# Loading the first rows of a position table on a second DMA ring, beside the indices of an embedding gather

## The chip, the core and the metric

The kernel runs on one core of a Trainium2 chip. A core has a matrix engine (PE), VectorE (DVE), ScalarE (ACT), GpSimd (POOL) and SyncE (SP), and 16 DMA engines that move data between HBM and on-chip memory. SyncE, ScalarE and GpSimd can each issue DMAs; here each of the three has a ring (queue) of its own, which feeds the same 16 DMA engines.

The metric is device time in microseconds (us) of one launch. Kernels are compared only with runs of the kernel before on the same chip.

## The reference

```python
batch, seq_len, vocab_size, d_model = 32, 512, 50000, 512
def reference(indices, embedding_table, position_embed):
    return (embedding_table[indices] + position_embed).astype(np.float32)
```

There are 32 x 512 = 16384 rows of 2 KB to gather, add to and store: 33.55 MB in and 33.55 MB out. The positions (1.05 MB) and the indices (0.13 MB) are small beside that.

## The kernel before

A batch of 512 positions lies as 128 partitions x 4 rows (`k` = 0 to 3), so one indirect DMA gathers 128 rows, 256 KB, with one index per partition. There are 128 gathers. The first 16 (batches 0 to 3) take their indices from a small tile, `idx0`, that is loaded directly; they run in the order of all `k` = 0, 1 first, then all `k` = 2, 3. The later ones take theirs from a transposed tile that the engines make meanwhile. VectorE adds the positions, which ScalarE has copied to PSUM, and SyncE stores.

```python
    # SyncE: loads, then (below) all stores
        nc.sync.dma_start(out=idx0[:], in_=idx_first).then_inc(s_first, 16)   # 16 KB
        load_pos(0)                                  # k = 0, 1: 512 KB
        nc.sync.wait_ge(s_pos[0], 16)
        load_pos(1)                                  # k = 2, 3: 512 KB
        nc.sync.dma_start(out=idx_raw[:], ...).then_inc(s_raw, 16)            # 128 KB
    # GpSimd
        nc.gpsimd.wait_ge(s_first, 16)
        for g, (b, k) in enumerate(order):
            # ... (waits for the transposed indices and for free slots)
            ins = nc.gpsimd.indirect_dma_start(
                out=slots[b % SLOTS][:, k, :], ..., in_=table,
                in_offset=bass.IndirectOffsetOnAxis(ap=where, axis=0),
            ).then_inc(s_gather[g % LANES], 16)
    # VectorE, for each gather (cut)
            if b == 0:
                nc.vector.wait_ge(s_ps, k + 1)
            nc.vector.tensor_tensor(out=part, in0=part, in1=pos_ps[:, k, :], op=add
            )._wait_ge(s_gather[g % LANES], rounds(g)).then_inc(s_add, 1)
    # ScalarE
        for k in range(K):
            nc.scalar.copy(out=pos_ps[:, k, :], in_=pos_sb[:, k, :])._wait_ge(
                s_pos[k // half], 16).then_inc(s_ps, 1)
    # SyncE: stores of 512 KB (two k of a batch), waiting on s_add
```

## Time and profile before

| | kernel before |
|---|---|
| time, median of 3 runs | 183.18 us (183.13 to 183.28) |
| the profiled run | 177.2 us, span 175.5 us (6 us under the timed runs) |
| first gather starts | 3.31 us |
| last gather starts | 162.31 us |
| gathers | 128, one every 1.25 us |
| busy share | GpSimd 69%, VectorE 51%, DMA engines over 90% nearly throughout |

These are whole lines from the page of the profile. The first three are by slice: each digit or number is one of 40 equal slices of the span, in tenths of busy time or in GB/s. The last two are the chain of waits that ended last, by engine and by line of the program.

```profile
POOL 4777777777777777777777777777777777777200
DMA  4799999999999999999999999999999999999993
GB/s 120 234 316 309 349 383 402 390 410 410 416 412 418 416 419 419 418 418 418 416 421 418 420 418 420 418 418 419 418 416 417 420 418 418 418 419 418 418 413 130
...
POOL 66%; issue 24%; DMA 5%; POOLq 1%; DVE 0%; SPq 0%
POOL slot L131 66%; DMA slot<-in_embedding_table_dram,idx_t 4%; DMA idx<-in_indices_dram 1%; POOLq L139 1%; DVE slot L166 0%; POOLq L126 0%; SPq L211 0%; SPq L103 0%
```

The last gather in that chain, from its start to its landing (start, duration, what):

```profile
162.31 7.63 DMA slot<-in_embedding_table_dram,idx_t
```

The timeline of the head, before. Columns: start, duration, engine ("SPq" is a DMA being issued by SyncE), line, operation, out<-in, count, and in brackets how long the engine sat idle before it and what ended that.

```profile
1.02 0.43 SPq L105 DMA_DIRECT2D idx<-in_indices_dram  x1
1.52 3.83 SPq L99 DMA_DIRECT2D pos_sb<-in_position_embed_dram  x2
3.31 1.14 POOL L131 DMA_INDIRECT slot<-in_embedding_table_dram,idx  x1 [1.72 <-DMA idx<-in_indices_dram]
5.03 1.11 ACT L172 COPY pos_ps<-pos_sb 128x512 f32<-128x512 f32 x2 [2.77 <-DMA pos_sb<-in_position_embed_dram]
6.79 0.69 DVE L166 TENSOR_TENSOR slot<-slot,pos_ps 128x512 f32<-128x512 f32 x1 [6.79 <-DMA slot<-in_embedding_table_dram,idx]
...
10.85 0.69 DVE L166 TENSOR_TENSOR slot<-slot,pos_ps 128x512 f32<-128x512 f32 x1 [3.37 <-DMA slot<-in_embedding_table_dram,idx]
```

The first gather waits for the indices alone. The positions, behind them on the same ring, arrive while the gather is under way: the first add (6.79) waits for the gather, not for them.

### The profile page before, as it was taken

How to read it: one execution, taken by the hardware profiler on the slowest of the kernel's cores; microseconds unless marked ns; L12 is line 12 of the kernel's file. 1: busy time of each engine (PE TensorE's matmuls, PEld its weight loads, DVE VectorE, ACT ScalarE, POOL GpSimd, SP SyncE). 2: the span in 40 equal slices, each digit the busy share in tenths (PEclk: the TensorE clock that was granted, in tenths of full speed). 3: DMA queues.
4: the chain of work that ended last, by engine and by line, in shares of the span. 5: the costliest groups of instructions: out<-in, count | busy, mean ns of one | idle time of the engine just before them, and what ended most of it. 6: DMA issues, size and time to landing. Idle time of an engine off the chain costs nothing.

```text
span 175.5 us, 423 instructions
## 1 busy us (share of the span) xinstructions
PE 1.0 (1%) x4; PEld 0.4 (0%) x4; DVE 89.1 (51%) x133; ACT 3.5 (2%) x5; POOL 121.9 (69%) x134
## 2 busy tenths in 40 slices
PE   0000100000000000000000000000000000000000
PEld 0000000000000000000000000000000000000000
DVE  0136645555465556465545554565455645554550
ACT  2220000000000000000000000000000000000000
POOL 4777777777777777777777777777777777777200
DMA  4799999999999999999999999999999999999993
GB/s 120 234 316 309 349 383 402 390 410 410 416 412 418 416 419 419 418 418 418 416 421 418 420 418 420 418 418 419 418 416 417 420 418 418 418 419 418 418 413 130
DMA packets 20851, 68.34 MB, mean 389 GB/s; under 512 B 3696, under 2 KB 3824, under 8 KB 20848
## 3 DMA queue, kind: packets, MB, share of 16 engines
q1 hardware_dynamic: 10608, 34.76, 49.0%
q0 software_dynamic: 10240, 33.56, 49.0%
q14 instruction: 3, 0.02, 0.0%
HBM read 34.75 MB, written 33.55 MB: 389 GB/s over the span
## 4 chain that ended last, share of the span: by engine, by line
POOL 66%; issue 24%; DMA 5%; POOLq 1%; DVE 0%; SPq 0%
POOL slot L131 66%; DMA slot<-in_embedding_table_dram,idx_t 4%; DMA idx<-in_indices_dram 1%; POOLq L139 1%; DVE slot L166 0%; POOLq L126 0%; SPq L211 0%; SPq L103 0%
## 5 line engine op out<-in xcount | busy, mean ns | idle before, releaser
L131 POOL DMA_INDIRECT slot<-in_embedding_table_dram,idx_t x112 | 105.9, 946 | 34.1 <-issue 34.1
L166 DVE TENSOR_TENSOR slot<-slot,pos_ps 128x512 f32<-128x512 f32 x128 | 87.9, 688 | 81.5 <-DMA slot<-in_embedding_table_dram,idx_t 63.6
L131 POOL DMA_INDIRECT slot<-in_embedding_table_dram,idx x16 | 15.3, 958 | 6.3 <-issue 4.6
L172 ACT COPY pos_ps<-pos_sb 128x512 f32<-128x512 f32 x4 | 2.2, 586 | 8.0 <-DMA pos_sb<-in_position_embed_dram 8.0
L172 ACT ACT_TABLE_LOAD x1 | 1.3, 1283 | 1.0 <-SPq L103 1.0
L160 DVE CAST idx_t<-turned 32x128 int32<-32x128 f32 x4 | 1.1, 279 | 0.1
L144 PE MATMUL turned<-ident,idx_f 128*32 128x128 f32 x4 | 1.0, 416 | 17.2 <-DVE idx_f L154 17.2
L114 POOL MEMSET ones<- 128x128 f32 x1 | 0.2, 204 | 0.5 <-SPq L103 0.5
L144 PEld LDWEIGHTS turned<-ident,idx_f 128*32 128x32 f32 x4 | 0.4, 133 | 17.3 <-DVE idx_f L154 17.2
L115 POOL TENSOR_SCALAR_AFFINE_SELECT ident<-ones 128x128 f32<-128x128 f32 x1 | 0.3, 287 | 0.1
L200 POOL MEMSET const-float32-0.0<- 128x1 f32 x1 | 0.1, 98 | 0.3 <-issue 0.3
L154 DVE CAST idx_f<-idx_raw 128x128 f32<-128x128 int32 x1 | 0.2, 220 | 0.0
L200 POOL MEMSET const-uint8-127<- 128x1 uint8 x1 | 0.1, 115 | 0.0
L200 POOL MEMSET const-bfloat16-1.0<- 128x1 bf16 x1 | 0.1, 109 | 0.0
L200 POOL MEMSET const-float32-1.0<- 128x1 f32 x1 | 0.1, 101 | 0.0
## 6 DMA issues: line engine op xcount, KB each, us to landing
out_dram<-slot SPq DMA_DIRECT2D x61, 512.0 KB, 6.6
slot<-in_embedding_table_dram,idx_t POOLq DMA_INDIRECT x112, 7.4
out_dram<-slot SPq DMA_DIRECT2D x6, 256.0 KB, 3.9
pos_sb<-in_position_embed_dram SPq DMA_DIRECT2D x2, 512.0 KB, 4.9
slot<-in_embedding_table_dram,idx POOLq DMA_INDIRECT x16, 6.3
idx_raw<-in_indices_dram SPq DMA_DIRECT2D x1, 128.0 KB, 6.2
idx<-in_indices_dram SPq DMA_DIRECT2D x1, 16.0 KB, 2.0
```

Of the source, the lines that this page charges most:

```text
L114: nc.gpsimd.memset(ones[:], 1.0).then_inc(s_ident, 1)
L115: nc.gpsimd.affine_select(out=ident[:], in_=ones[:], pattern=[[-1, P]], compare_op=mybir.AluOpType.is_equal, fill=0.0, base=0, channel_mul ...
L131: ins = nc.gpsimd.indirect_dma_start(out=slots[b % SLOTS][:, k, :], out_offset=None, in_=table, in_offset=bass.IndirectOffsetOnAxis(ap=whe ...
L139: nc.gpsimd.drain()
L144: ins = nc.tensor.transpose(turned[:, k].rearrange("p b j -> p (b j)"), idx_f[:, :, k], ident[:])
L154: nc.vector.tensor_copy(out=idx_f[:].rearrange("r p k -> r (p k)"), in_=idx_raw[:, :, 0])._wait_ge(s_raw, 16).then_inc(s_cast, 1)
L160: nc.vector.tensor_copy(out=idx_t[j * Q : (j + 1) * Q, :, :], in_=turned[:, :, :, j]).then_inc(s_idx, 1)
L166: nc.vector.tensor_tensor(out=part, in0=part, in1=pos_ps[:, k, :], op=add)._wait_ge(s_gather[g % LANES], rounds(g)).then_inc(s_add, 1)
L172: nc.scalar.copy(out=pos_ps[:, k, :], in_=pos_sb[:, k, :])._wait_ge(s_pos[k // half], 16).then_inc(s_ps, 1)
L200: nc = _bacc.Bacc("TRN2", target_bir_lowering=False, num_devices=1)
```

## The change

The intent: start the first gather sooner, by gating it on a quarter of the early indices; take the first positions off SyncE's ring so that they go out at the same moment; spread the later positions; and move the raw indices ahead of them.

```diff
-        if (b == 0 and k < half) or b == B - 1:
+        if (b <= 1 and k < half) or b == B - 1:
             stores.append((g + 1, b, k, 1))
...
-        nc.sync.dma_start(out=idx0[:], in_=idx_first).then_inc(s_first, 16)
-        load_pos(0)
-        nc.sync.wait_ge(s_pos[0], 16)
-        load_pos(1)
+        for k in range(half):
+            load_pos(nc.scalar, k)
+        nc.sync.dma_start(out=idx0[:, 0, :], in_=idx_first[:, 0, :]).then_inc(
+            s_first, 16
+        )
+        nc.sync.dma_start(out=idx0[:, 1:, :], in_=idx_first[:, 1:, :]).then_inc(
+            s_next, 16
+        )
         nc.sync.dma_start(
             out=idx_raw[:], in_=idx_rows.rearrange("r (s w) -> r s w", w=2)
         ).then_inc(s_raw, 16)
+        nc.sync.wait_ge(s_pos[half - 1], 16)
+        load_pos(nc.sync, half)
+        nc.sync.wait_ge(s_gather[0], 16)
+        load_pos(nc.sync, half + 1)
...
         for g, (b, k) in enumerate(order):
+            if g == half:
+                nc.gpsimd.wait_ge(s_next, 16)
```

(`load_pos` now takes an engine and one `k`, 256 KB, and ScalarE's copies wait for one semaphore per `k`.)

## The prediction

> **What bounds the kernel.** The page's DMA rows: the 16 DMA engines are at least 90% busy from the third of 40 slices to the last but one, at about 418 GB/s once settled. Bytes (34.75 MB read, 33.55 MB written) are the least the task allows, but for 1.2 MB of positions and indices. GpSimd keeps the same pace: in the timeline a gather starts every 1.25 us (0.95 busy, 0.30 "issue"), and 256 KB in plus 256 KB out per 1.25 us is 419 GB/s. The chain of waits names GpSimd (66%, issue 24%), but the last gather, issued at 162.31, takes 7.63 us to land where the quickest took 3.5 (DMA view of the gather line), so some 4 us of transfers are queued: DMA bounds the end, GpSimd is nearly level. Nothing between 20 and 170 us can gain. The head can: by slice it moves 120, 234, 316, 309, 349, 383 GB/s. Against 418 these slices of 4.39 us lose about 8.4 us, over 2 of them before any data moves.
>
> **What the change does.**
> 1. Only batch 0's indices (4 KB, not 16 KB) gate the first gather. Before, all took 2.01 us to land and the gather started at 3.31. The quarter should land sooner, but two 256 KB position loads now go out on ScalarE's ring at the same moment (ScalarE was free at 0.97, SyncE at 1.02). The Trainium skill ("DMA: Bandwidth & Descriptors", Issuing engines are not separate DMA queues) says that DMAs of different issuers share the same 16 engines and interleave; before issues every load from SyncE, so its trace cannot show this. The effects should nearly cancel: first gather 0.2 us earlier, between 0.5 earlier and 0.4 later.
> 2. Positions 0 and 1 no longer queue behind the indices (one SyncE issue: 0.43 us): the first ScalarE copy moves from 5.03 to about 4.2. It gates nothing: the first add waited until 6.79 for gather 0.
> 3. Raw indices (128 KB) move ahead of the later positions and fill the hole between the first positions and the first gather's data (DMA share 0.48 from 4 to 6 us), worth 0.3 to 0.5 us of transfers.
> 4. Positions 2 and 3 come as two 256 KB loads, the second after gather 0. Before, 512 KB plus 128 KB stood beside gathers 1 to 3: gather 1 (issued 4.75) was added only at 10.85. Now that add should come near 9. Batch 1's first pair is stored in two pieces, so writes mix with reads about 2 us sooner.
>
> Costs: three more DMAs (0.43 us of issue each, off the chain) and 2 KB packets instead of 4 KB for 1.5 MB. VectorE, TensorE and the gathers are unchanged.
>
> **Sum.** Only DMA idleness removed in the first 12 us counts: 0.4 (hole) + 0.2 (earlier gather) + 0.3 (earlier stores) = 0.9 us, an estimate. The end moves as much, since the queue of 4 us shrinks without emptying.
>
> **Predicted:** 182.3 us, 8 in 10 between 181.2 and 183.3. Faster by over 2%: 0.03; within 2%: 0.95; slower by over 2%: 0.02.
>
> **Signs.** First gather near 3.1; gather pace still 1.25; second add near 9; second slice above 234 GB/s; settled slices still 418; last gather's latency about 7 us.
>
> **What would make it wrong.** Position packets hold up the index slice (first gather after 3.5): no gain. If the timed runs, 6 us longer than the profiled one (177.2), spend that in the head, the gain could be larger; if GpSimd alone sets the end, only the first gather's shift counts.

## The result

| | before | changed |
|---|---|---|
| time, median of 4 runs each, same rounds | 183.16 us | 184.75 us |
| ratio | | 1.0085 (95% interval 1.0068 to 1.0103) |
| first gather starts (profile) | 3.31 us | 4.53 us |
| last gather starts | 162.31 us | 163.50 us |
| last data moved by a DMA engine | 173.15 us | 174.03 us |

A ratio is the mean time of one kernel's fast runs over the mean of the other's fast runs of the same rounds, so it is not quite the ratio of the medians quoted beside it. The change is a small loss, within 2% but clear of noise, and outside the predicted range of 181.2 to 183.3.

The page's lines after the change:

```profile
POOL 1877777777777777877877877877877777760000
DMA  4689999999999999999999999999999999999700
GB/s 143 178 282 351 368 368 367 397 410 412 416 418 418 415 422 418 417 425 416 418 423 415 419 422 413 424 418 417 424 415 418 424 416 420 421 415 423 298 2 0
...
POOL 60%; issue 23%; DMA 6%; DVE 4%; POOLq 1%; SPq 0%
```

The slices are longer here (183.7 us in 40 parts), because this profile ends with 9.7 us in which nothing moves; the zeros on the right are that end. It is no part of the change, as the runs below show. The settled rate is the same, about 418 GB/s. What differs is the left edge, GpSimd's 1 where it had 4.

The timeline of the head, after:

```profile
0.97 0.88 ACTq L98 DMA_DIRECT2D pos_sb<-in_position_embed_dram  x2
1.02 0.38 SPq L107 DMA_DIRECT2D idx<-in_indices_dram  x1
1.47 0.42 SPq L110 DMA_DIRECT2D idx<-in_indices_dram  x1
...
4.10 1.29 ACT L182 COPY pos_ps<-pos_sb 128x512 f32<-128x512 f32 x2 [0.93 <-DMA pos_sb<-in_position_embed_dram]
4.53 1.14 POOL L141 DMA_INDIRECT slot<-in_embedding_table_dram,idx  x1 [2.94 <-DMA idx<-in_indices_dram]
...
7.93 0.59 ACT L182 COPY pos_ps<-pos_sb 128x512 f32<-128x512 f32 x1 [2.55 <-DMA pos_sb<-in_position_embed_dram]
...
8.53 0.69 DVE L176 TENSOR_TENSOR slot<-slot,pos_ps 128x512 f32<-128x512 f32 x1 [8.53 <-ACT pos_ps L182]
...
9.86 0.69 DVE L176 TENSOR_TENSOR slot<-slot,pos_ps 128x512 f32<-128x512 f32 x1 [0.64 <-DMA slot<-in_embedding_table_dram,idx]
```

The view names ScalarE's copy as what released the first add at 8.53. By the program that add needs only the first copy, which was done by 4.7; the copy that ended at 8.52 is the third (`k` = 2). So it is the gather that the add waited for, as the repeat of this kernel says (e5, add at 8.33).

The index load is a quarter of the size and takes longer. One line of the chain of waits from each kernel, before and then after, gives it (start, duration, what):

```profile
1.02 2.01 DMA idx<-in_indices_dram
```

```profile
1.02 3.22 DMA idx<-in_indices_dram
```

The packet records of the two traces (one record for each piece that a DMA engine moves) show why. They were counted per quarter microsecond over all 16 DMA engines, by the ring's number and the record's size: 32 bytes are indices, 2048 and 4096 bytes are positions.

```
start (us)   before: SyncE's ring alone       changed: SyncE's ring | ScalarE's ring
1.94         49 x 32 B                                              | 14 x 2048 B
2.19         350 x 32 B                       4 x 32 B              | 16 x 2048 B
2.44         113 x 32 B,  5 x 4096 B          20 x 32 B             | 24 x 2048 B
2.69                     11 x 4096 B          32 x 32 B             | 28 x 2048 B
2.94                     19 x 4096 B          33 x 32 B             | 34 x 2048 B
3.19                     22 x 4096 B          26 x 32 B             | 41 x 2048 B
3.44                     18 x 4096 B          15 x 32 B             | 43 x 2048 B
```

Before, all 512 index records were gone in about 0.6 us and the positions followed, in order. After, the 128 records of the small slice come out between those of the positions, in the middle nearly one for one, for 1.3 us: by the start of the 128th, 194 position records of 2 KB had started. (Records of the second slice look the same, so this is the 128th on the ring.) These counts mix 16 engines, which the records do not name, but the nanoseconds show the turns: of the first 128 index records, 83 start 3 or 4 ns before a 2 KB record ends and have another 2 KB record start 5 or 6 ns after them. With the index times shifted by eight amounts between 17 and 60 ns, chance gives 6 to 23. An index record takes 7 to 9 ns; the 2 KB records beside it take 87 to 154 ns on average, and the slice has to wait through one at about two steps in three. The Trainium skill says, in "DMA: Bandwidth & Descriptors", Queues, rings and completion order, that each DMA engine goes round-robin between the rings that have work for it. This trace agrees as to taking turns. Turns are not the whole delay: the first index record itself comes later, at 2.35 and after 23 position records, where in the kernel before it started at 2.10. In e2 that part is larger.

So there is a theory with two steps. First, the position packets on the second ring hold up the index slice by over a microsecond. Second, the start of the first gather passes to the end nearly in full, because GpSimd then issues one gather per 1.25 us to the end: from first to last gather it takes 159.00 us before and 158.97 us after.

The rivals: the loss comes from the other parts (2 KB records, gated later loads, one store cut in two); or the ring on ScalarE is itself slow; or the delayed slice just shares bandwidth with all bytes in flight; and, against the second step, the DMA engines bound the end, as the prediction had it.

### The profile page after: what moved, and what is told of

Its sections match the earlier page's. It is cut to its first block, busy times and chain, and to the rows that moved or that the text cites. A ratio compares the mean times of both kernels' runs of the same rounds, so it can differ in the third digit from the quotient of the medians.

```text
span 183.7 us, 427 instructions
## 1 busy us (share of the span) xinstructions
PE 1.0 (1%) x4; PEld 0.4 (0%) x4; DVE 89.2 (49%) x133; ACT 3.6 (2%) x5; POOL 121.9 (66%) x134
## 4 chain that ended last, share of the span: by engine, by line
POOL 60%; issue 23%; DMA 6%; DVE 4%; POOLq 1%; SPq 0%
POOL slot L141 60%; DMA slot<-in_embedding_table_dram,idx_t 4%; DVE slot L176 4%; DMA idx<-in_indices_dram 2%; POOLq L149 1%; POOLq L136 0%; SPq L221 0%; SPq L102 0%
```

## The experiments

Twelve kernels ran, each on one chip with 11 runs of the kernel before beside them. "us" is (ratio - 1) times the median of before on that chip (177.58, 183.38 and 177.16 us); the gather's shift is against the 3.31 us of the first profile.

| run | first gather (us) | shift | ratio to before, 95% interval | us |
|---|---|---|---|---|
| e1 ScalarE waits for the slice | 3.00 | -0.31 | 0.9990 (0.9947 to 1.0033) | -0.2 |
| e2 before, only the ring changed | 5.04 | +1.73 | 1.0101 (1.0060 to 1.0141) | +1.8 |
| e3 before, only the slice split | 3.08 | -0.23 | 0.9977 (0.9940 to 1.0015) | -0.4 |
| e4 before again | 3.33 | +0.02 | 0.9986 (0.9945 to 1.0026) | -0.2 |
| e5 change again | 4.32 | +1.01 | 1.0065 (1.0049 to 1.0082) | +1.2 |
| e6 slice ahead on the same ring | 2.94 | -0.37 | 0.9992 (0.9973 to 1.0010) | -0.1 |
| e7 before, gather held back | 5.85 | +2.54 | 1.0137 (1.0115 to 1.0159) | +2.5 |
| e8 change without small stores | 4.49 | +1.18 | 1.0066 (1.0049 to 1.0083) | +1.2 |
| e9 half the positions beside | 4.20 | +0.89 | 1.0054 (1.0019 to 1.0090) | +1.0 |
| e10 short position records | 3.45 | +0.14 | 1.0028 (0.9986 to 1.0070) | +0.5 |
| e11 before, 512 KB less | 3.18 | -0.13 | 1.0012 (0.9970 to 1.0054) | +0.2 |
| e12 e6 again, another chip | 2.90 | -0.41 | 0.9970 (0.9933 to 1.0006) | -0.5 |

In every row the two columns, shift and us, agree within 0.4 us, in e11 too, which moves less data. The intervals are 0.3 to 0.8 us wide to each side, so this is as close as they can show.

### e1: ScalarE waits for the index slice

```diff
+        nc.scalar.wait_ge(s_first, 16)
         for k in range(half):
             load_pos(nc.scalar, k)
```

> The changed kernel, but ScalarE issues its two position loads only when the first index slice has landed. Theory (position packets on ScalarE's ring hold up the index slice): slice lands in under 2.0 us, first gather at or below 3.1 us in the profile instead of 4.53, and the run is at least 1.2 us faster than the changed kernel, so 183.5 us or less, at or below the kernel before. Rival (the loss comes from the smaller position loads, their gates or the extra small stores, the late gather being absorbed by the queue of transfers): gather early all the same, but time stays at 184.3 us or more.

```profile
3.00 1.14 POOL L142 DMA_INDIRECT slot<-in_embedding_table_dram,idx  x1 [1.42 <-DMA idx<-in_indices_dram]
```

The first gather started at 3.00 us. The chip was another than the first one, with before at 177.58, so the absolute numbers of the expectation could not be read; against before the run came to 0.9990, where the change stands at 1.0065 to 1.0085. The ring, the smaller loads, their gates and the small stores are all still there, so none of them is the loss.

### e2: the kernel before with its first positions on ScalarE's ring

```diff
-        load_pos(0)
+        load_pos(0, nc.scalar)
```

> The kernel before, with one edit: its first 512 KB position load goes out on ScalarE's ring, not behind the indices on SyncE. Theory: the 16 KB of indices now interleave with position packets, 32 descriptors a DMA engine against 8 of 4 KB; first gather after 4.0 us instead of 3.31, time 0.6 to 1.5 us above the kernel before. Rival (smaller loads, gates, small stores): none of these is here, so time within 0.3 us of the kernel before.

This one edit alone costs 1.8 us, slightly more than the expectation's upper end of 1.5. The gather starts at 5.04, later than in the changed kernel, since four times as many index records wait:

```profile
5.04 1.14 POOL L131 DMA_INDIRECT slot<-in_embedding_table_dram,idx  x1 [3.46 <-DMA idx<-in_indices_dram]
```

The last index record started at 4.41 us, after all 128 position records of 4 KB: 16 KB of indices came in behind 512 KB of positions although the two were issued within 0.05 us of each other (positions by ScalarE at 0.98, indices by SyncE at 1.02).

Taking turns is only part of it here. The first index record starts at 3.09, after 74 of the position records, where in the kernel before it started at 2.10. So 0.99 of the gather's 1.73 us are gone before the first turn. Why the second ring comes in so late, and later beside 4 KB records than beside 2 KB ones (2.35 in the changed kernel), is open; no run tried it.

### e3: the kernel before with the slice split off

```diff
-        nc.sync.dma_start(out=idx0[:], in_=idx_first).then_inc(s_first, 16)
+        nc.sync.dma_start(out=idx0[:, 0, :], in_=idx_first[:, 0, :]).then_inc(s_first, 16)
+        nc.sync.dma_start(out=idx0[:, 1:, :], in_=idx_first[:, 1:, :]).then_inc(s_next, 16)
...
+            if g == half:
+                nc.gpsimd.wait_ge(s_next, 16)
```

> The kernel before, with one edit: batch 0's indices (4 KB) are loaded by themselves ahead of those of batches 1 to 3, all on SyncE ahead of the positions. Theory: first gather at 2.9 to 3.1 us instead of 3.31, time 0.1 to 0.5 us below the kernel before. Rival (the start of the first gather does not set the end): gather as early, time the same within 0.1 us.

The gather starts 0.23 us sooner, and the ratio of 0.9977 has 1 in its interval. The part of the change that was meant to help does move the gather, by too little to be seen in the time on this chip.

### e4: the kernel before, again

> The kernel before, unchanged, as a control: ratio 1.000 within 0.002. Its profiled run of before was 177.2 us where its other runs were 183.1, and the changed kernel's profile ends with 9.6 us in which no data moves. If that slow end is in every ordinary run and the first profile just missed it, this profile shows some 8 us after the last store here too; if it comes from the change, it does not.

Ratio 0.9986, as a control should be. Its profile shows no slow end (span 175.1 us, last data at 172.90), but all runs of this chip were near 177 us, so this could not answer the question about the end. That answer came from e6 and e12.

### e5: the change, again

> The changed kernel unchanged, as a control beside the kernel before on one chip. First gather at 4.4 to 4.6 us as before; 0.7 to 1.7 us slower than the kernel before (the prediction's own run said 1.6). On a chip without the slow end its span ends within 2.5 us of the last store, so that the end is no part of the change.

Ratio 1.0065, 1.2 us slower, with the gather at 4.32, a little below the expected 4.4. This ran on a chip whose runs of before are at 183.4 us, and the slow end was there again (span 183.4, last data at 174.11), so the part of the expectation about the end went untested here.

### e6: the slice ahead of the positions on one ring

```diff
+        nc.scalar.dma_start(out=idx0[:, 0, :], in_=idx_first[:, 0, :]).then_inc(
+            s_first, 16
+        )
         for k in range(half):
             load_pos(nc.scalar, k)
-        nc.sync.dma_start(out=idx0[:, 0, :], in_=idx_first[:, 0, :]).then_inc(
-            s_first, 16
-        )
```

> The changed kernel with one edit: the first index slice is issued on ScalarE's ring ahead of the two position loads, not on SyncE beside them; no wait is added. Theory (packets of two rings take turns, those of one ring go in order): slice lands at about 2.7 us, first gather at 2.9 to 3.1, positions at 4.5 to 5.0, time 1 us or more below the changed kernel and at or up to 0.8 us below the kernel before. Rival (the ring or the hardware issue on ScalarE is itself slower): first gather stays at 4 us or later.

```profile
0.97 0.42 ACTq L105 DMA_DIRECT2D idx<-in_indices_dram  x1
1.43 0.94 ACTq L98 DMA_DIRECT2D pos_sb<-in_position_embed_dram  x2
...
2.94 1.14 POOL L141 DMA_INDIRECT slot<-in_embedding_table_dram,idx  x1 [1.35 <-DMA idx<-in_indices_dram]
4.52 0.59 ACT L182 COPY pos_ps<-pos_sb 128x512 f32<-128x512 f32 x1 [0.84 <-DMA pos_sb<-in_position_embed_dram]
```

One moved DMA, no wait added, and the loss is gone: 183.36 us against 184.69 for the change on the same chip. The slice went out on ScalarE's ring, so that ring is not slow in itself. The slice's 128 records start from 2.02 to 2.32, and the first position record at 2.53. Two things changed at once, though: the slice is ahead on the same ring, and the positions are issued 0.46 us after it (1.43 against 0.97). A head start of that size with the positions on another ring might do as well; no run separates the two. The positions still arrive before they are wanted (first copy at 4.52, first add at 6.64).

This run also tests the prediction's item 3. In the two microseconds from 4 to 6 the DMA engines' share and rate (the last two columns of the view by windows) were, before, after and in e6:

```profile
4.00:6.00 2.00, 0.00 (x0) 0.00 (x0) 0.00 (x0) 0.97 (x2) 1.40 (x2) 1.00 0.48 147
```

```profile
4.00:6.00 2.00, 0.00 (x0) 0.00 (x0) 0.00 (x0) 1.18 (x2) 1.17 (x2) 1.00 0.36 98
```

```profile
4.00:6.00 2.00, 0.00 (x0) 0.00 (x0) 0.00 (x0) 1.12 (x2) 1.39 (x3) 1.00 0.93 297
```

In e6 the hole is filled, as item 3 wanted, and there is no gain of 0.3 to 0.5 us to show for it.

### e7: the kernel before with its first gather held back

```diff
         nc.gpsimd.wait_ge(s_first, 16)
+        nc.gpsimd.wait_ge(s_pos[0], 16)
```

> The kernel before with one edit: GpSimd also waits for the first position load, so the first gather starts near 5.3 us instead of 3.3 and no DMA is changed or moved by it. Theory (the start of the first gather passes to the end nearly in full): 1.5 to 2.1 us slower than the kernel before, like the run with the positions alone on ScalarE's ring (gather at 5.04, 1.7 us slower). Rival (the queue of transfers absorbs a late start; the loss there came from the DMA order): under 0.7 us slower.

```profile
5.85 1.14 POOL L132 DMA_INDIRECT slot<-in_embedding_table_dram,idx  x1 [4.26 <-DMA pos_sb<-in_position_embed_dram]
```

The wait held the gather to 5.85, half a microsecond past the 5.3 expected. Start 2.54 us later, time 2.5 us longer (4 runs), so the time too lies past the expected 2.1: a late start is passed on in full, with every load left as it was.

### e8: the change without its small stores

```diff
-        if (b <= 1 and k < half) or b == B - 1:
+        if (b == 0 and k < half) or b == B - 1:
```

> The changed kernel with one edit: batch 1's first pair is stored as one 512 KB DMA again. Theory: within 0.4 us of the changed kernel, since the loss is in the first gather. Rival (2 KB packets and an extra store cost it): 0.7 us or more faster than the changed kernel.

Ratio 1.0066 against 1.0065 for the change on the same chip. The small stores cost nothing and bring nothing that can be seen (the intervals are 0.3 us wide to each side).

### e9: half as many position bytes beside the slice

```diff
-        for k in range(half):
-            load_pos(nc.scalar, k)
+        load_pos(nc.scalar, 0)
+        nc.scalar.wait_ge(s_first, 16)
+        load_pos(nc.scalar, 1)
```

> The changed kernel with one edit: ScalarE issues its second 256 KB position load only after the first index slice has landed, so 256 KB stand beside the slice, not 512 KB. Theory (taking turns packet by packet: the slice's 8 descriptors a DMA engine alternate with the first load's 8, so the second load was not yet in play): the slice still lands with position 0, first gather at 4.1 to 4.5 us, time within 0.4 us of the changed kernel. Rival (the slice shares bandwidth with everything in flight): half the bytes, half the delay, first gather near 3.6, time 0.5 us or more below the changed kernel.

```profile
4.20 1.14 POOL L142 DMA_INDIRECT slot<-in_embedding_table_dram,idx  x1 [2.62 <-DMA idx<-in_indices_dram]
```

Half the bytes, nearly the whole delay. A share of bandwidth would have brought the gather to about 3.6; taking turns leaves it at 4.20, against 4.32 to 4.53 with both loads. The second load mattered a little, then, not in proportion.

### e10: the same position bytes in shorter records

```diff
-        for k in range(half):
-            load_pos(nc.scalar, k)
+        for q in range(4):
+            at = slice(q * D // 4, (q + 1) * D // 4)
+            nc.scalar.dma_start(out=pos_sb[:, 0, at], in_=pos_rows[:, 0, at]
+            ).then_inc(s_pos[0], 16)
+        load_pos(nc.scalar, 1)
```

> The changed kernel with one edit: position 0 is loaded on ScalarE's ring in four 64 KB quarters, so that the descriptors taking turns with the slice are 512 bytes, not 2 KB. Theory (one position packet passes for each index packet): a turn costs a quarter or a third, slice landed by about 3.1 us, first gather at 3.0 to 3.4, time 0.8 us or more below the changed kernel. Rival (merely using two rings, or bytes in flight, delays the slice): first gather stays at 4.1 us or later.

```profile
0.98 1.85 ACTq L107 DMA_DIRECT2D pos_sb<-in_position_embed_dram  x4
...
3.45 1.14 POOL L145 DMA_INDIRECT slot<-in_embedding_table_dram,idx  x1 [1.86 <-DMA idx<-in_indices_dram]
```

Two rings and an unordered slice as in the change, but 512-byte records of about 28 ns to take turns with, and the gather starts at 3.45, about a microsecond sooner, just past the expected 3.0 to 3.4. The time's interval (0.9986 to 1.0070) is too wide to confirm a gain of 0.8 us; the delay of the slice is what this run settles. One caveat: ScalarE also spaces the four loads 0.46 us apart, so fewer bytes stand in its ring at a time. E9 says that bytes alone matter little.

### e11: the kernel before with 512 KB less to move

```diff
-        load_pos(1)
...
-            nc.scalar.copy(out=pos_ps[:, k, :], in_=pos_sb[:, k, :])._wait_ge(
-                s_pos[k // half], 16
+            nc.scalar.copy(out=pos_ps[:, k, :], in_=pos_sb[:, k % half, :])._wait_ge(
+                s_pos[0], 16
```

> The kernel before without its second position load (positions 2 and 3 are copied from 0 and 1: a wrong result on purpose). 512 KB less to move, 1.25 us at 418 GB/s, the first gather starts as before at 3.3. If transfers bound the end, as the prediction had it: 1.0 to 1.4 us faster than the kernel before. If the end follows from the first gather's start and GpSimd's pace of one gather per 1.25 us: at most 0.4 us faster.

The result is wrong on purpose: positions 2 and 3 are not loaded. The packets did shrink:

```profile
DMA packets 20851, 68.34 MB, mean 389 GB/s; under 512 B 3696, under 2 KB 3824, under 8 KB 20848
```

```profile
DMA packets 20707, 67.82 MB, mean 386 GB/s; under 512 B 3680, under 2 KB 3808, under 8 KB 20704
```

```profile
3.18 1.14 POOL L130 DMA_INDIRECT slot<-in_embedding_table_dram,idx  x1 [1.60 <-DMA idx<-in_indices_dram]
```

```profile
162.20 8.12 DMA slot<-in_embedding_table_dram,idx_t
```

(packets before, then in e11; first and last gather in e11). The time did not: ratio 1.0012, with the lower end of the interval at 0.9970, a gain of 0.5 us at most, where 1.25 us of transfers were taken away. This separates the two things that e7 leaves together. Bytes in the head can be removed without a gain, so the DMA engines' work there does not set the end. One caveat: this profile is at the higher of two levels of a gather's time (8.0 us in the middle against 7.4 before; see the last section), which the timed runs do not show; if e11 met that level more often than before did, part of a gain could hide in it.

### e12: the slice ahead, again

> The index slice ahead of the positions on ScalarE's ring, once more, to see whether it beats the kernel before: its first gather starts 0.37 us earlier. Theory (the start passes on in full): 0.2 to 0.5 us faster. Rival (the early part of that is lost again before the transfers settle): same within 0.2 us.

Ratio 0.9970 with an interval of 0.9933 to 1.0006. All four runs with an early gather (e1, e3, e6, e12) lie 0.1 to 0.5 us under before, where the theory says 0.2 to 0.4, but each interval holds 1. That e6 beats the change is shown; that it beats the kernel before is not.

It also settles the slow end. It is the same program as e6, on another chip: there the last data moved at 172.87 us and the span was 182.2; here at 173.60 and 175.8. The 9.3 us of silent end against 2.2 us belong to the chip and to no kernel: all four profiles of e6's chip end with 9.0 to 9.3 us of silence, all eight of the other two with 2.2 to 2.4.

## Why the prediction was wrong

**The first failed step is item 1, "The effects should nearly cancel: first gather 0.2 us earlier, between 0.5 earlier and 0.4 later."** The mechanism was named: the loads interleave on the same 16 engines. Its size was not. The slice's own gain is 0.23 us (e3); the holding up by positions came to 1.22 us net of that in the profile, 1.01 in the repeat. The prediction gave no sum for it, only a range that ended at 0.4 us later. In these runs turns are taken by record, so a small load of many short records waits through about as many long ones of the other ring (e9, e10), after a late start of its first record that stays unexplained (e2). The prediction had named this as what would make it wrong, "Position packets hold up the index slice (first gather after 3.5): no gain". The condition held; the consequence was a loss, not a missing gain.

**The second failed step is the sum, "Only DMA idleness removed in the first 12 us counts."** It read two facts, DMA engines over 90% busy and a last gather that takes 7.6 us where the quickest took 3.5, as a backlog that earlier transfers would shorten. E11 removed 1.25 us of transfers and gained nothing, and its last gather still took 8.1 us from its start to its add. In all profiles the middle gathers take 7.3 to 8.4 us (medians), whatever the head was like. This fits a time that a gather takes in the settled mix, and not work left over from the head; what sets it was not tried. What holds is the alternative named last in the prediction: only the first gather's shift counts. The chain of waits had named GpSimd ("POOL 66%; issue 24%").

**What that makes of the 0.9 us.** The 0.4 for the hole was worth nothing that can be seen (e6 filled it). The 0.3 for earlier stores was worth nothing either: the second add did come earlier, 9.86 against 10.85, in a slower kernel, and taking the extra small store out again changed nothing (e8). The 0.2 for an earlier gather became 1.22 later. The sum with the right terms is the shift alone, +1.0 to +1.2 us, and the two measurements of the change are +1.2 us (e5) and +1.6 us (the first result). The interval of the first result begins at 1.25 us (0.0068 of 183.16), so some tenths of a microsecond of it are not explained by the shift of 1.22 in its one profile.

**What was right.** The first copy on ScalarE at "about 4.2" came at 4.10, and it gates nothing: the first add starts 3.8 us after that copy's end. The pace of the gathers stayed at 1.25 us, settled slices at about 418 GB/s, and the last gather at 7.24 us from its start to its add. The time stayed within 2%. Three signs failed: the first gather near 3.1 (4.53), the second add near 9 (9.86), and the second of the profile's 40 slices above 234 GB/s (178).

## What to carry to other kernels

A small load that something waits for is badly placed beside a bulk load that another ring issues at the same moment (e2: 1.8 us). Put it ahead of the bulk on the same ring (e6), or let the bulk wait for it (e1). When an engine that issues work at a fixed pace lies on the chain from its first instruction to its last, price a change of the head by what it does to that first instruction, and test "the DMA engines are full" by taking bytes away (e11) before building a sum of transfers on it.

## What the Trainium skill lacked or had wrong

- "DMA: Bandwidth & Descriptors", Queues, rings and completion order, says that a DMA engine drains a whole packet of about 9 to 17 descriptors from one ring before it switches. Here the two rings alternated record by record: 83 of the first 128 index records stand within nanoseconds between two 2 KB records (chance gives 6 to 23), and 194 records of 2 KB had started by the start of the 128th, counted over all 16 engines; in e9 it was 111. It also lacks the late start of the second ring: 0.99 us to its first record beside 4 KB records (e2).
- The same page, Issuing engines are not separate DMA queues, says that issuing from several engines "will only save the time on the sequencer". It lacks the cost: a bulk load moved to another ring no longer stays behind the small one that something waits for. That alone was 1.8 us in e2.
- "Perfetto Trace Analysis", Identifying the Most-Contended Engine, says to find the most-contended engine by occupancy, and DMA by HBM utilization. Here DMA engines were above 90% busy at 418 GB/s, GpSimd at 69%, and yet 512 KB less of transfers gained nothing (ratio 1.0012) while a later first gather cost its whole delay (2.54 us, 2.5 us). It lacks the test by removal.
- No page has that the end of a program can take longer on one chip than on another (nearest is "Runtime: NRT & Kernel Launch", The ~15µs preamble/postamble breakdown): the same kernel spent 2.2 us after its last data on one chip and 9.3 us on another (e12, e6), which more than covers the difference between times near 177 and near 183 us. In the changed kernel's trace five of SyncE's closing instructions take 0.70 to 1.40 us each, where before's take 0.01 to 0.03; why is open.
- No page has the two levels of a gather's time in the settled stretch: in the median of gathers 40 to 99, from issue to add, 7.3 to 7.5 us in nine of the fourteen profiles and 8.0 to 8.4 us in five, the same kernel showing both (7.42 in e6, 8.43 in e12). What decides it was not tried.
